# Third token group before the prompt in every stage of an encoder layer, and the prompt's FFN operands kept in DRAM

## The chip, the cores and the metric

The kernel runs on one core of a Trainium2 chip. The metric is the device time of one execution in microseconds (us). Three runs of the kernel before gave 1874.11, 1875.97 and 1880.21 us (median 1875.97 us); the execution that was profiled took 1872.49 us. The engines are named as the profile names them: PE is TensorE (matmul; PEld its weight load), DVE is VectorE, ACT is ScalarE, POOL is GpSimd, SP is SyncE, which issues nearly all DMAs.

## The reference, cut to what matters

One encoder layer with the same weights is applied to a prompt of 1024 tokens and to a sample of 512 tokens; a conditioning vector of each gives its six adaLN vectors. Width is 1024, FFN width 2816, everything in float32.

```
def encoder_layer(x, c, ...):
    mod = silu(c) @ w_ada + b_ada                  # six vectors: sh1 sc1 gt1 sh2 sc2 gt2
    h = rms_norm(x, g_pre_mix) * (1 + sc1) + sh1
    proj = h @ w_in                                # q, k, v of 12 heads x 64; gu, gv of 256 each
    for three dilations (1, 4, 16), 4 heads each:  # 64 strided neighbours on each side, ALiBi
        out[g], lse[g] = dilated_window_attention(q, k, v)
    attn = concat(softmax over g of lse[g] * out[g])
    gm = gelu(gu) * (w_s @ layer_norm(gelu(gv)) + b_s)     # in chunks of 128 positions
    x = x + gt1 * rms_norm(concat(attn, gm) @ w_out, g_post_mix)
    h = rms_norm(x, g_pre_ffn) * (1 + sc2) + sh2
    gate, up = split(h @ w_gu)
    return x + gt2 * rms_norm((silu(gate) * up) @ w_down, g_post_ffn)
```

## The kernel before, in words

Tokens are handled in three groups of 512: groups 0 and 1 are the two halves of the prompt (`self.P`), group 2 is the sample (`self.S`). Activations lie transposed, as 8 chunks of 128 channels by 512 tokens. Every float32 operand of a matmul is split in a high and a low part: `split` (lines 139 to 141) copies on ACT and subtracts on DVE or POOL, and `mm3` does three matmuls for each 128 channels (high by high, high by low, low by high). So a tile of 128 output channels for one group is 24 matmuls of 128x512. Weights come from DRAM through 4 buffers `wraw` and are split into 4 buffers `whl`; one tile's weights take two of each, so that one tile can be prepared ahead. Activations come through 3 buffers `xc` (`load_chunk`). The split activations `h` of a group take 8 of 16 buffers.

The stages of the kernel before run in this order (`run`, lines 1132 to 1204). Statistics of group 0, the first two adaLN vectors (`ada_first`). The prompt's attention slot 0 (`attention_slot`: nine tiles, q, k and v of three dilations, of half of the heads), with the first four tiles' matmuls taken chunk by chunk as `h` of group 0 comes (`project_first`); `gmlp` of groups 0 and 1 (v product, GELU and normalisation on ACT, DVE and POOL, u product, position mixing); the prompt's attention slot 1; the sample's two attention slots; the output projections of groups 0 and 1 (`out_proj`); `gmlp(2)`; the output projection of group 2. Then the prompt's FFN: its up projection (`ffn_up`) multiplies both halves with Strassen-like block products, seven for every 128 hidden channels (`wino_products`), whose right operands are sums and differences of the halves' `h` (called B11, T2, B21, T3, T1, T4, B22). `wino_in` makes them while `out_proj(2)` runs, keeps five of them split in SBUF and two in DRAM (`late`), which `wino_late` brings back. `ffn_down` of groups 0 and 1 follows, and at the end the sample's FFN with plain products (`ffn`, `down`).

Work off the matmul path is written as generators in the list `self.back`; `tick(n)` advances it n steps between tiles, `tick(-1)` empties it. It holds softmax and the value products of a slot (`behind` in `attention_slot`), `mix_in` (loads the mixed outputs of a group and their reciprocal denominators `rden`, multiplies, splits on POOL), the normalisation and residual behind an output projection (`post`), `modulate` (makes `h`). `post` of an FFN that is not the last one sums squares over partitions with `rms_slow` (POOL, then ten instructions on DVE). The last stage has its own ending (`post_last`, lines 888 to 905), which works in halves of the tokens. A scheduler of the framework fixes each engine's order of instructions ahead of the run; on each engine they then run in that order.

Of the kernel before, what the change touches and what calls it, by code (L numbers as in the profile page):

```python
# [9 lines left out]
F32 = mybir.dt.float32  # L10
# [68 lines left out]
class Layer:  # L79
    def __init__(self, tc, ctx, a):  # L80
# [14 lines left out]
        self.late = self.dr.tile([2, 4, 128, TG], F32, name="late")  # L95
# [334 lines left out]
    def project_first(self, grp, tiles, steps):  # L430
# [17 lines left out]
        for hf, gi in enumerate(grp.halves):  # L448
            for i, (w, (_, evac, after)) in enumerate(zip(ws, tiles)):
                if hf:  # L450
                    ps[i] = self.p("mm")
                    self.mm3(ps[i], w, range(KC), self.h[gi])
                self.flush()
                with self.tc.high_priority(offset=1):
                    evac(hf, ps[i])
                if hf:
                    self.tick(steps)
                    self.pending.append(after)
# [259 lines left out]
    def attention_slot(self, grp, sp, steps, between=None, start=None):  # L718
# [22 lines left out]
        if grp is self.P and sp == 0:  # L741
# [3 lines left out]
        if grp is self.P and sp == 0:  # L745
# [90 lines left out]
    def post(self, gi, product, G, xsrc, dst, follow, steps):  # L836
# [3 lines left out]
        last = gi == NG - 1 and not follow  # L840
# [47 lines left out]
    def post_last(self, sq, ys, product, G, xsrc, dst):  # L888
# [4 lines left out]
        for i, ps in enumerate(product(KC - 1, True)):  # L893
            o = slice(256 * i, 256 * i + 256)
            with self.tc.high_priority(offset=1):
                nc.scalar.activation(ys[-1][:, 1, o], ps, AF.Copy, scale=G[:, KC - 1, 1:2])
# [33 lines left out]
    OPS = ["vm"] * 2 + ["v"] * 3 + ["qk"] * 3 + ["sc"] + ["qk"] * 3 + ["h"] * 8  # L930
    HIDP = ["h"] * 8 + ["qk"] * 6 + ["v"] * 3 + ["vm"] * 2 + ["sc"] + ["st"] * 2
# [4 lines left out]
    def wino_in(self, ops):  # L936
# [3 lines left out]
        for o in ("B11", "T2", "B21", "T3", "T1", "T4", "B22"):  # L940
            ops[o] = []
        for k in range(4):
            B = {}
            for kk in range(2):
                pair = self.t("st", [128, 2, 512])
                for gi in range(2):
                    kc = k + 4 * kk
                    x = self.load_chunk(self.x1[gi, :, kc])
                    t = pair[:, gi]
                    nc.vector.tensor_tensor(out=t, in0=x, in1=rs[gi], op=ALU.mult)  # L950
# [325 lines left out]
```

## Time and profile before

| | us |
|---|---|
| runs, median (lowest to highest) | 1875.97 (1874.11 to 1880.21) |
| the profiled execution | 1872.49 |
| its span, first to last instruction | 1870.4 |
| PE busy | 1797.6 (96%) |
| DVE busy | 1051.6 (56%) |
| ACT busy | 692.3 (37%) |
| POOL busy | 123.6 (7%) |
| mean granted clock of TensorE | 0.981 |

The span and the time differ by 2.1 us outside the instructions. PE is busy in 96% of the span, so a reader looks first at where it is not (the stretches with less than 50 us of PE in 50), then at the clock in the same stretches: at 0.5 a matmul takes twice its time and PE still counts as busy.

### The profile page before, as it was taken

The page shows a single profiled execution, that of the slowest core. Times are in us where ns is not written, and L with a number is a line of the kernel's source. Part 1 is how long each engine was busy: PE and PEld are TensorE (multiplying, and loading weights), DVE is VectorE, ACT ScalarE, POOL GpSimd, SP SyncE. Part 2 cuts the span into 40 slices and gives each one's busy share as a digit, 9 for nine tenths or more (in the row PEclk, how much of TensorE's full clock was granted, in tenths as well). Part 3 has the DMA queues.
Part 4 walks back from the last instruction along what each step waited for, and adds up shares of the span by engine and source line. Part 5 has one row for each costly group of instructions (what it writes and reads, how often), then busy time and mean ns, then how long its engine had stood idle before and what let it go on. Part 6 is the DMA issues. An engine that isn't in the chain of part 4 may idle for free.

```text
span 1870.4 us, 22825 instructions
## 1 busy us (share of the span) xinstructions
PE 1797.6 (96%) x8442; PEld 1406.2 (75%) x8442; DVE 1051.6 (56%) x1663; ACT 692.3 (37%) x1196; POOL 123.6 (7%) x82
## 2 busy tenths in 40 slices
PE   6899999999999977889999999999999999999997
PEld 3677876767777866667778888877887888888886
DVE  3424963573675566985566766663375374444223
ACT  4511642162334545642332322343345333333232
POOL 0000100010131003400000000000002000000001
PEclk9899999999999998889999999999999999999999
DMA  9012332233363446553322222264365252222432
GB/s 365 29 56 71 106 114 76 81 129 131 102 202 129 143 164 196 182 201 108 118 94 71 79 91 73 74 205 142 100 209 184 95 170 92 95 96 93 138 93 76
DMA packets 126127, 232.44 MB, mean 124 GB/s; under 512 B 14144, under 2 KB 19520, under 8 KB 126016
## 3 DMA queue, kind: packets, MB, share of 16 engines
q1 hardware_dynamic: 125872, 230.93, 37.0%
q8 instruction: 66, 1.08, 0.2%
q14 instruction: 45, 0.37, 0.1%
q10 hardware_dynamic: 144, 0.07, 0.0%
HBM read 196.86 MB, written 34.08 MB: 123 GB/s over the span
## 4 chain that ended last, share of the span: by engine, by line
PE 51%; issue 3%; DVE 2%; DMA 1%; ACT 0%; POOL 0%; DVEq 0%; POOLq 0%; ACTq 0%
PE pmm L158 44%; PE ppv L158 6%; DMA xc<-hid 1%; PE pst L158 1%; DVE h L141 0%; DVE sc L902 0%; DVE whl L141 0%; DVE sc L861 0%; DMA xc<-late 0%; DVE sc L904 0%; POOL h L141 0%; ACT h L140 0%; DVE v L141 0%; DVE st L1026 0%; DVE qk L141 0%
## 5 line engine op out<-in xcount | busy, mean ns | idle before, releaser
L158 PE MATMUL pmm<-h,whl 128*128 128x512 f32 x3717 | 921.7, 400 | 11.9 <-ACT h L140 6.3
L158 PEld LDWEIGHTS pmm<-h,whl 128*128 128x128 f32 x3717 | 692.4, 190 | 204.1 <-issue 27.4
L141 DVE TENSOR_TENSOR whl<-wraw,whl 128x512 fp32r<-128x512 f32 (+1 forms) x420 | 291.6, 699 | 302.4 <-ACT whl L140 302.1
L140 ACT CAST whl<-wraw 128x512 fp32r<-128x512 f32 (+1 forms) x420 | 252.8, 606 | 495.8 <-PE pmm L158 353.9
L158 PE MATMUL pmm<-qk,whl 128*128 128x512 f32 x798 | 201.7, 397 | 1.2 <-DVE whl L141 1.2
L158 PEld LDWEIGHTS pmm<-qk,whl 128*128 128x128 f32 x798 | 151.0, 190 | 37.2 <-DVE whl L141 2.4
L158 PE MATMUL pmm<-h,sc 128*128 128x512 f32 x411 | 103.8, 397 | 0.0
L158 PE MATMUL ppv<-h,whl 128*128 128x512 f32 x396 | 100.0, 395 | 0.0
L158 PE MATMUL pmm<-v,whl 128*128 128x512 f32 x342 | 90.4, 396 | 0.9 <-ACT whl L140 0.9
L158 PEld LDWEIGHTS pmm<-h,sc 128*128 128x128 f32 x411 | 78.4, 192 | 17.1 <-DVE h L141 0.6
L158 PEld LDWEIGHTS ppv<-h,whl 128*128 128x128 f32 x396 | 74.5, 188 | 18.1 <-issue 0.8
L158 PE MATMUL pst<-qk 64*128 64x128 f32 (+3 forms) x384 | 69.4, 334 | 17.8 <-DVE qk L141 17.5
L158 PEld LDWEIGHTS pst<-qk 64*128 64x128 f32 (+1 forms) x384 | 50.8, 199 | 39.3 <-issue 32.8
L158 PEld LDWEIGHTS pmm<-v,whl 128*128 128x128 f32 x342 | 64.2, 188 | 18.1 <-ACT whl L140 3.0
L158 PE MATMUL pmm<-vm,whl 128*128 128x512 f32 x225 | 65.5, 407 | 4.9 <-ACT whl L140 4.9
L192 DVE TENSOR_TENSOR acc<-acc,ta 128x512 f32<-128x512 f32 x55 | 38.8, 705 | 49.4 <-ACT ta L849 42.7
L140 ACT CAST whl<-sd 128x512 fp32r<-128x512 f32 x53 | 32.7, 619 | 87.2 <-PE ppv L158 52.1
L158 PEld LDWEIGHTS pmm<-vm,whl 128*128 128x128 f32 x225 | 42.4, 192 | 20.9 <-ACT whl L140 6.9
L218 POOL TENSOR_TENSOR rq<-rq,half 128x4 f32<-128x4 f32 (+1 forms) x11 | 12.0, 1091 | 623.1 <-DVE rq L217 623.1
L141 DVE TENSOR_TENSOR whl<-sd,whl 128x512 fp32r<-128x512 f32 x53 | 36.5, 688 | 21.8 <-ACT whl L140 21.7
L848 ACT ACTIVATE sc<-pmm,G 128x512 f32<-128x512 f32 x47 | 32.3, 688 | 41.9 <-PE pmm L158 41.8
L1026 DVE TENSOR_TENSOR st<-st,ppv 128x512 f32<-128x512 f32 x44 | 30.1, 685 | 31.0 <-PE ppv L158 30.7
(249 smaller groups left out, 1929.3 us busy)
## 6 DMA issues: line engine op xcount, KB each, us to landing
wraw<-in_wgu SPq DMA_DIRECT2D x132, 256.0 KB, 2.5
wraw<-in_wdn SPq DMA_DIRECT2D x120, 256.0 KB, 2.6
wraw<-in_win SPq DMA_DIRECT2D x80, 256.0 KB, 2.8
xc<-in_wada SPq DMA_DIRECT2D x48, 256.0 KB, 3.3
wraw<-in_wout SPq DMA_DIRECT2D x48, 256.0 KB, 3.0
sd<-in_wgu SPq DMA_DIRECT2D x44, 256.0 KB, 3.3
xc<-hid SPq DMA_DIRECT2D x44, 256.0 KB, 3.3
xc<-in_x SPq DMA_DIRECT2D x40, 256.0 KB, 3.4
```

The lines of the kernel that those rows point to most:

```text
L140: self.nc.scalar.copy(hi, src)
L141: (eng or self.nc.vector).tensor_tensor(out=lo, in0=src, in1=hi.bitcast(F32), op=ALU.subtract)
L158: self.nc.tensor.matmul(out, lhsT, rhs, start=start, stop=stop, skip_group_check=True)
L192: nc.vector.tensor_tensor(out=acc, in0=acc, in1=t, op=ALU.add)
L218: nc.gpsimd.tensor_tensor(out=y, in0=y, in1=self.half8[:, :n], op=ALU.pow)
L848: nc.scalar.activation(ys[-1][:, mt % 2], ps, AF.Copy, scale=G[:, mt, c:c + 1])
L1026: add = lambda o, a, b: nc.vector.tensor_tensor(out=o, in0=a, in1=b, op=ALU.add)
```

## The change

The sample comes first in each stage. `run` now goes: the sample's slot 0 (with `project_first`), `gmlp(2)`, the sample's slot 1, the prompt's slots 0 and 1, `gmlp(0)`, `gmlp(1)`, the output projections of groups 2, 0 and 1, the sample's FFN, the prompt's `ffn_up`, `ffn_down(0)`, `ffn_down(1)`, which is now the last stage. `wino_in` and `wino_late` become `operands`, which runs in `self.back` during the sample's FFN and stores all seven operands in DRAM (`ops`), and `operands_in`, which loads and splits them: two operands during the sample's down projection, five between it and `ffn_up`. In the prompt's slot 0 the first two tiles, not the last two, are taken together, and `h` of group 1 is finished between their halves (`second_half`). The number of matmuls of each shape is the same.

```diff
@@ project_first
-        for hf, gi in enumerate(grp.halves):
-            for i, (w, (_, evac, after)) in enumerate(zip(ws, tiles)):
...
+        for p, (_, evac, after) in zip(ps, tiles):
+            self.flush()
+            with self.tc.high_priority(offset=1):
+                evac(0, p)
+            self.tick(steps)
+            self.pending.append(after)
@@ attention_slot
         if between:
-            tiles[-2:] = [tiles[-2] + tiles[-1]]
+            tiles[:2] = [tiles[0] + tiles[1]]
         for t in tiles:
-            self.project(grp, t, steps, between if t is tiles[-1] else None)
+            self.project(grp, t, steps, between if t is tiles[0] else None)
@@ post
-        last = gi == NG - 1 and not follow
+        last = gi == 1 and not follow
@@ 
-    OPS = ["vm"] * 2 + ["v"] * 3 + ["qk"] * 3 + ["sc"] + ["qk"] * 3 + ["h"] * 8
+    OPS = ["h"] * 8 + ["v"] * 3 + ["qk"] * 6 + ["vm"] * 2 + ["sc"] + ["h"] * 8
...
-    def wino_in(self, ops):
+    def operands(self):
         rs = [self.spread(self.rs2[gi], True) for gi in range(2)]
+        yield
         for k in range(4):
...
+            a, b = self.t("sd", [128, 3, 512]), self.t("sd", [128, 3, 512])
+            B = {(0, 0): a[:, 0], (0, 1): a[:, 1], (1, 0): a[:, 2], (1, 1): b[:, 0]}
+            for (kk, gi), t in B.items():
+                nc.sync.dma_start(out=t, in_=self.x1[gi, :, k + 4 * kk])
+            yield
+            for (kk, gi), t in B.items():
+                kc = k + 4 * kk
+                nc.vector.tensor_tensor(out=t, in0=t, in1=rs[gi], op=ALU.mult)
+                nc.scalar.activation(t, t, AF.Identity, bias=self.mod[:, 3, kc, 0:1], scale=self.G[2][:, kc, 0:1])
+                if gi:
+                    yield
+            B11, B12, B21, B22, T1, T2 = a[:, 0], a[:, 1], a[:, 2], b[:, 0], b[:, 1], b[:, 2]
+            keep = lambda o, t: nc.sync.dma_start(out=self.ops[o, k], in_=t)
             self.sub(T1, B12, B11)
             self.sub(T2, B22, T1)
+            keep(0, B11)
...
+    def operands_in(self, ops, os):
+        for o in os:
             for k in range(4):
-                x = self.load_chunk(self.late[i, k])
-                h = self.t("h", [128, 2, 512], F32R)
+                x = self.load_chunk(self.ops[o, k])
+                h = self.t(self.OPS[4 * o + k], [128, 2, 512], F32R)
                 self.split(h[:, 0], h[:, 1], x)
                 ops[o].append(h)
+                yield
@@ ffn
-            self.tick(1)
+            self.tick(2)
+        self.back.append(self.operands_in(ops, range(2)))
         self.down(gi, hid)
@@ run
+        self.attention_slot(self.S, 0, STEPS[0], start=start)
+        self.gmlp(2, GS)
+        self.alongside(self.x_stats_behind(self.chunks(self.a["x"][1]), rs, 1))
+        self.attention_slot(self.S, 1, STEPS[1])
+        while 1 not in rs:
+            self.tick(1)
+        self.alongside(self.make_h(1, rs[1], self.chunks(self.a["x"][1]), H2))
+        self.attention_slot(self.P, 0, STEPS[2], second_half)
+        self.attention_slot(self.P, 1, STEPS[3])
         hs = [[], [], []]
+        self.gmlp(0, GS)
+        self.alongside(self.mix_in(2, hs[2]))
+        self.gmlp(1, GS)
+        while len(hs[2]) < KC:
+            self.tick(1)
+        self.back.append(self.mix_in(0, hs[0]))
+        self.out_proj(2, hs[2], 4)
...
+        self.alongside(self.mix_in(1, hs[1]))
+        self.out_proj(0, hs[0], 3)
...
+        self.back.insert(0, self.ffn_in(2, h2))
+        self.out_proj(1, hs[1], 3)
...
+        self.back.append(self.operands())
+        self.ada = self.ada_rest((5,))
+        self.ffn(2, h2, ops)
+        while len(ops[1]) < 4:
+            self.tick(1)
+        for _ in self.operands_in(ops, range(2, 7)):
+            pass
+        self.ffn_up(ops)
+        self.ffn_down(0)
+        self.ffn_down(1)
         self.tick(-1)
```

The change moves instructions on every engine. Three places are shown: first PE at the last gMLP ahead of an output projection. Before, that is `gmlp(2)`; `pmm<-whl,h` is its v product, `pmm<-h,whl` x48 its u product, `pst<-qk` its position mixing, and the next `pmm<-h,whl` the projection of group 2. Before:

```order
L158 MATMUL pmm<-whl,h 128x256 x30
L158 MATMUL pst<-tb,ones 128x128 x4
L158 MATMUL pmm<-h,whl 128x512 x48
L158 MATMUL pst<-qk 128x128 x32
L158 MATMUL pmm<-h,whl 128x512 x8
```

On PE in the changed program, the same place is `gmlp(1)`; `ppv` are value products of the prompt's slot 1.

```order
L158 MATMUL pmm<-h,whl 128x512 x46
L158 MATMUL ppv<-sc,v 64x192 x2
L158 MATMUL ppv<-sc,v 64x256 x4
L158 MATMUL ppv<-sc,v 64x192 x2
L158 MATMUL pst<-qk 128x128 x16
L158 MATMUL pmm<-h,whl 128x512 x9
L158 MATMUL ppv<-sc,ones_82 64x64 x2
L158 MATMUL ppv<-sc,ones_82 64x192 x2
L158 MATMUL ppv<-sc,ones_82 64x256 x4
L158 MATMUL ppv<-sc,ones_82 64x192
L158 MATMUL pst<-qk 128x128 x16
```

Value products and the first matmuls of an output projection now stand between the u product and the position mixing.

The second place is DVE where one pair of attention slots ends and `h` of a group must replace that of the group before it: `L387` and `h<-tb,h` make `h`, `whl` are weight splits. Before, at the end of the prompt's slots:

```order
L141 TENSOR_TENSOR whl<-wraw,whl 128x512 x2
L141 TENSOR_TENSOR h<-tb,h 128x512
L387 TENSOR_TENSOR tb<-xc,rs 128x512
L141 TENSOR_TENSOR h<-tb,h 128x512
L387 TENSOR_TENSOR tb<-xc,rs 128x512
```

On DVE in the changed program, between the sample's slot 1 and the prompt's slot 0; `L589` is the maximum over keys and `L618` the subtraction of it in the softmax of the sample's slot 1:

```order
L141 TENSOR_TENSOR h<-tb,h 128x512
L493 SCALAR_TENSOR_TENSOR sc<-cst,pst 128x512
L387 TENSOR_TENSOR tb<-xc,rs 128x512
L618 TENSOR_TENSOR sc<-sc,st 128x64
L589 TENSOR_TENSOR st<-st,sc 128x4x128
L618 TENSOR_TENSOR sc<-sc,st 128x3x128 x2
L618 TENSOR_TENSOR sc<-sc,st 128x64
L618 TENSOR_TENSOR sc<-sc,st 128x512 x2
L141 TENSOR_TENSOR h<-tb,h 128x512
L141 TENSOR_TENSOR whl<-wraw,whl 128x512
```

The softmax of the slot just ended now stands among the instructions that make `h`, ahead of a weight split.

The third place is DVE at the head of `ffn_up`: `whl` are the split weights of the block products, `x<-xc,x` the split operands. Before, where the two late operands are split:

```order
L141 TENSOR_TENSOR whl<-wraw,whl 128x512 x2
L141 TENSOR_TENSOR whl<-ta,whl 128x512
L141 TENSOR_TENSOR h<-sd,h 128x512
L934 TENSOR_TENSOR wraw<-wraw 128x512
L141 TENSOR_TENSOR h<-st,h 128x512
L934 TENSOR_TENSOR st<-st,sd 128x512
L141 TENSOR_TENSOR h<-xc,h 128x512 x2
```

On DVE in the changed program, at the same place; the split in the first row is that of the first block product's weights, the one in the last row holds the second's:

```order
L141 TENSOR_TENSOR whl<-wraw,whl 128x512
L141 TENSOR_TENSOR qk<-xc,qk 128x512 x3
L141 TENSOR_TENSOR vm<-xc,vm 128x512 x2
L929 TENSOR_TENSOR ta<-wraw 128x512
L141 TENSOR_TENSOR sc<-xc,sc 128x512
L986 TENSOR_TENSOR wraw<-wraw 128x512
L192 TENSOR_TENSOR acc<-acc,ta 128x512
L141 TENSOR_TENSOR h<-xc,h 128x512
L929 TENSOR_TENSOR wraw<-wraw 128x512
L141 TENSOR_TENSOR h<-xc,h 128x512 x2
L141 TENSOR_TENSOR whl<-wraw,whl 128x512 x2
```

Fifteen of the twenty operand chunks that come in from DRAM now stand ahead of the second product's weights (the six rows before these hold the other six).

## Rows read from the trace of the kernel before

**Rows 1.** The page, busy time, share and instructions of each engine.

```profile
PE 1797.6 (96%) x8442; PEld 1406.2 (75%) x8442; DVE 1051.6 (56%) x1663; ACT 692.3 (37%) x1196; POOL 123.6 (7%) x82
```

**Rows 2.** Windows: stretch, its length, busy us of engines, PE clock, DMA share, GB/s.

```profile
0.00:50.00 50.00, 33.52 (x154) 16.87 (x154) 18.96 (x51) 21.80 (x39) 1.45 (x8) 0.96 0.90 341
...
650.00:700.00 50.00, 40.44 (x234) 35.11 (x232) 32.97 (x58) 25.51 (x51) 3.66 (x3) 0.94 0.51 172
700.00:750.00 50.00, 39.17 (x164) 30.46 (x165) 35.52 (x55) 29.11 (x53) 16.93 (x13) 0.82 0.61 192
750.00:800.00 50.00, 39.95 (x162) 30.79 (x160) 46.55 (x67) 33.17 (x61) 21.36 (x10) 0.90 0.59 193
800.00:850.00 50.00, 47.16 (x184) 34.98 (x185) 38.91 (x65) 18.00 (x31) 1.32 (x1) 0.90 0.55 189
...
900.00:950.00 50.00, 50.00 (x224) 38.32 (x223) 31.28 (x60) 16.79 (x29) 0.00 (x0) 1.00 0.33 111
...
1600.00:1650.00 50.00, 50.00 (x217) 40.54 (x216) 20.78 (x32) 16.10 (x27) 0.00 (x0) 1.00 0.27 95
```

**Rows 3.** Waits of PE: on whom, us in total, times, longest.

```profile
PE pst L158 <- DVE qk L141: 17.5, 2, 13.0
...
PE pst L158 <- DVE acc L192: 6.4, 1, 6.4
PE pmm L158 <- ACT h L140: 6.3, 4, 3.9
```

**Rows 4.** Timeline of PE: start, us, instructions, idle before and its end.

```profile
71.35 13.72 PE L158 MATMUL pmm<-h,whl 128*128 128x512 f32 x48 [3.94 <-ACT h L140]
...
679.03 11.41 PE L158 MATMUL pmm<-h,whl 128*128 128x512 f32 x48
703.40 3.64 PE L158 MATMUL pst<-qk 128*128 128x128 f32 x16 [12.96 <-DVE qk L141]
...
801.55 1.22 PE L158 MATMUL pmm<-vm,whl 128*128 128x512 f32 x2 [4.14 <-ACT whl L140]
804.06 5.49 PE L158 MATMUL pmm<-h,whl 128*128 128x512 f32 x12 [1.28 <-DVE st L1026]
```

**Rows 5.** Windows of 10 and 30 us, columns as in rows 2.

```profile
20.00:30.00 10.00, 7.69 (x28) 3.10 (x28) 8.04 (x20) 6.29 (x12) 0.00 (x0) 0.83 1.03 410
...
680.00:710.00 30.00, 14.08 (x61) 11.59 (x60) 28.11 (x52) 15.20 (x28) 3.27 (x2) 0.74 0.60 199
```

**Rows 6.** Groups by form: line, engine, operation, count, busy us, mean ns, idle before.

```profile
L141 DVE TENSOR_TENSOR whl<-wraw,whl 128x512 fp32r<-128x512 f32 x396 | 281.8, 716 | 273.6 <-ACT whl L140 273.3
...
L862 DVE TENSOR_TENSOR sc<-sc,xc 128x512 f32<-128x512 f32 x40 | 26.9, 686 | 14.8 <-DMA xc<-x 8.4 <-DMA xc<-in_x 6.3
L861 DVE TENSOR_TENSOR sc<-sc,rs 128x512 f32<-128x512 f32 x40 | 24.6, 683 | 0.6 <-ACT rs L234 0.6
...
L623 DVE TENSOR_TENSOR sc<-sc,st 128x512 f32<-128x512 f32 x16 | 13.5, 888 | 0.0
L734 DVE RECIPROCAL st<-st 128x1024 f32<-128x1024 f32 x2 | 13.1, 6564 | 0.0
...
L594 DVE TENSOR_TENSOR st<-st,sc 128x512 f32<-128x512 f32 x8 | 9.1, 1157 | 0.1
...
L140 ACT CAST h<-xc 128x512 fp32r<-128x512 f32 x40 | 24.7, 619 | 44.7 <-DVE xc L912 26.6 <-DMA xc<-hid 8.1 <-DMA xc<-late 6.6
```

**Rows 7.** Tile xc, 1222 to 1266 us: issue ns (min/median/max), first and last start.

```profile
L239 SPq DMA_DIRECT2D xc<-hid x26: 319/320/326, 1225.0 to 1263.8; - x26
```

**Rows 8.** DMA issues: count, KB each, median us from issue to landing.

```profile
xc<-rden SPq DMA_DIRECT2D x18, 256.0 KB, 2.8
...
rden<-st SPq DMA_DIRECT2D x6, 256.0 KB, 2.0
```

**Rows 9.** Timeline of POOL: start, us, instructions, idle before and its end.

```profile
711.55 1.27 POOL L141 TENSOR_TENSOR h<-xc,h 128x512 fp32r<-128x512 f32 x1 [4.70 <-ACT h L140]
...
752.20 7.53 POOL L141 TENSOR_TENSOR qk<-st,qk 128x512 fp32r<-128x512 f32 x2 [4.31 <-ACT qk L140]
```

More of the change, by code (lines that the diff above doesn't have):

```diff
@@ L94, in __init__ @@
         self.hid = self.dr.tile([2, NJ, 128, TG], F32, name="hid")
-        self.late = self.dr.tile([2, 4, 128, TG], F32, name="late")
+        self.ops = self.dr.tile([7, 4, 128, TG], F32, name="ops")
         self.h = {}
@@ L740, in attention_slot @@
             tiles.append((9 * sp + 3 * g + 2, evac, after))
-        if grp is self.P and sp == 0:
+        if start:
             tiles = [tiles[i] for i in FIRST]
@@ L744, in attention_slot @@
         tiles = [[t] for t in tiles]
-        if grp is self.P and sp == 0:
+        if start:
             first = self.project_first(grp, [t[0] for t in tiles[:4]], steps)
@@ L1087, in ffn_in, with ffn @@
                                  0 if gi < 2 else 1, hs, H3)
-    def ffn(self, gi, h2):
+    def ffn(self, gi, h2, ops):
         nc = self.nc
@@ L1129, in by_halves @@
                 yield ps[:, 0:256]
-        self.post(gi, product, self.G[3], self.x1[gi], self.a["y"][gi], False, 2 if gi != 1 else 3)
+        self.post(gi, product, self.G[3], self.x1[gi], self.a["y"][gi], False, 2)
     def run(self):
@@ L1142, in run, with prepare @@
             self.raws.append(raw)
-        wa.append(self.ada_load(1))
-        load.append(self.resident(self.a["x"][1], ["v", "v", "v", "sc"]))
-        wa += [self.ada_load(2), self.ada_load(3)]
+        wa += [self.ada_load(ch) for ch in range(1, 4)]
         ada = self.ada_first(wa)
-        rs = {0: self.x_stats(load[0])}
+        rs = {2: self.x_stats(load)}
         for _ in ada:
             pass
+        def prepare(gi):
+            x = self.chunks(self.a["x"][gi])
+            yield from self.x_stats_behind(x, rs, gi)
+            yield from self.make_h(gi, rs[gi], x, H1)
         def start(first):
@@ L1167, in start @@
             self.ada = self.ada_rest((2, 3, 4))
-        def next_group():
-            self.alongside(self.make_h(2, rs[2], self.chunks(self.a["x"][2]), H2))
-            self.tick(NT)
-        for sp in range(2):
-            self.gmlp(sp, GS) if sp else None
-            if sp:
-                self.alongside(self.x_stats_behind(self.chunks(self.a["x"][2]), rs, 2))
-            self.attention_slot(self.P, sp, STEPS[0], next_group if sp else None, None if sp else start)
-            if not sp:
-                self.gmlp(0, GS)
@@ L1179, in run, with second_half @@
-        hs = [[], [], []]
-        for sp in range(2):
-            if sp:
-                self.back.append(self.mix_in(0, hs[0]))
-            self.attention_slot(self.S, sp, STEPS[1])
-        self.tick(-1)
-        self.back.append(self.mix_in(1, hs[1], tags=["qk"] * 6 + ["v"] * 2))
-        self.out_proj(0, hs[0], 4)
-        self.out_proj(1, hs[1], 4)
+            self.back.append(prepare(0))
+        def second_half():
+            while len(self.h[1]) < KC:
+                self.tick(1)
@@ new lines, in run @@
+        self.alongside(self.mix_in(2, hs[2]))
[4 more added lines that the diff above has]
+        self.out_proj(2, hs[2], 4)
+        while len(hs[0]) < KC:
+            self.tick(1)
+        self.alongside(self.mix_in(1, hs[1]))
+        self.out_proj(0, hs[0], 3)
+        while len(hs[1]) < KC or 2 not in self.rs2:
+            self.tick(1)
+        h2, ops = [], [[] for _ in range(7)]
+        self.back.insert(0, self.ffn_in(2, h2))
@@ L1188, in run @@
+        self.out_proj(1, hs[1], 3)
         for _ in self.ada:
             pass
-        self.back.append(self.mix_in(2, hs[2], range(6)))
-        self.gmlp(2, GS)
-        self.tick(-1)
-        for _ in self.mix_in(2, hs[2], range(6, 8)):
-            pass
-        ops, h2 = {}, []
-        self.back.append(self.wino_in(ops))
-        self.out_proj(2, hs[2], 3)
-        self.wino_late(ops)
-        self.ada = self.ada_rest((5,))
+        while len(h2) < KC:
+            self.tick(1)
+        self.back.append(self.operands())
```

80 lines of the change are left out of this document (19 added, 61 removed).

## The prediction

> **What bounds the kernel now.** Read the busy times first: PE is busy in 96% of the span, no other engine in more than 56% [rows 1]. The change leaves the matmuls as they are, so it can only move the time in which PE waits or runs at the half clock. The windows say where that is [rows 2]. From 850 us on PE fills every stretch at clock 1.00, as in 900 to 950; DVE then has 31.3 us of work in 50 in the prompt's `ffn_up`, 20.8 in the sample's FFN. The holes are two. At the start PE has 33.5 us in the first 50. Between 650 and 850 us it lacks 9.6 + 10.8 + 10.0 + 2.8 = 33.3 us, and the clock falls to 0.82.
>
> The waits and the timeline name what makes the second hole. In `gmlp(2)` PE finishes the u product at 679.03 + 11.41 = 690.4 us and has nothing queued that doesn't hang on the normalised v: it waits 13.0 us and again 4.5 (the pair is the 17.5 us of the waits) [rows 3, 4]. Meanwhile DVE is busy for 28.1 us of 30 [rows 5]: it also carries the residual of group 1. Then the head of `ffn_up`: 6.4 us for the square sum of `out_proj(2)`, 4.1 and 1.3 us for split weights [rows 3, 4].
>
> A wait costs more than itself. Behind the 4.1 and 1.3 us, twelve matmuls take 5.49 us, where 48 take 11.41 us at full clock, 2.85 us for twelve; behind the 3.94 us at the start, 48 take 13.72 us [rows 4]. So each gap of about 4 us adds some 2.5 us at half clock. For the five such places of the hole I take 13 us; clock times busy time in the four windows gives at most 2.4 + 7.1 + 4.0 + 4.7 = 18 us [rows 2].
>
> **What goes.** The middle hole, 33.3 + 13 = 46 us: `gmlp(1)` has value products and `out_proj(2)` beside its normalisation, `out_proj(2)` has `out_proj(0)` behind it, and the sample's FFN needs nothing that is made late, since its `h` comes during `out_proj(1)`. At the start, the 2 MB of group 1 no longer stand ahead of the last adaLN weights: at 410 GB/s [rows 5] 5 us. I count 2, since squares of group 0 and weight splits now stand on DVE ahead of the last two chunks of `h`. The wait for `h` of group 1 goes as well, 3.9 us and its 2.3 us of clock [rows 4]. Together 8 us. Gains: 54 us.
>
> **What comes.** Sums over DVE are made instruction by instruction in the changed order, with the durations of the groups (some stand in [rows 6]).
>
> Sample's slot 0 into `gmlp(2)`. Each weight tile now serves 24 matmuls, not 48, while DVE also makes statistics and `h` of group 0, scores and the softmax. Between the last full tile's weights and those of the v product DVE has 22 us of work; PE has 13 us, and 5.6 us of one prepared tile. Gap 3.5 us with clock 2.5: 6 us. Bounds: 0 (DVE was ahead) and 12 (the order's waits for POOL in the softmax fall in it).
>
> Sample's slot 1 into the prompt's slot 0. `h` of group 1 replaces that of group 2 while the softmax of slot 1 stands in the same order: from one half of the second tile's weights to the next lie about 15 us of DVE (the maxima at 1.16 us and the subtractions at 0.89 us are the long ones [rows 6]); PE has two half tiles of 5.6 us and about 5 us of slack. Gap 4, clock 2: 6 us, bounds 0 and 12.
>
> Head of `out_proj(0)`. Its second chunk needs the denominators of the prompt's slot 1. From the last value product: one addition 1.1, reciprocal 6.6, store 2.0, load 2.8, product 0.7, copy 0.6, subtraction on POOL 1.3, together 15 us [rows 6, 8, 9]. PE has two tiles of `out_proj(2)` and a chunk, 12.5 us: 2.5 us are missing. Six chunks follow, each with two loads through three `xc` buffers, about 2.8 us apart, where three tiles side by side give PE 2.1 us a chunk; 4.5 us more. With the clock 9.5 us; bounds 3 and 17.5 (the pair of `gmlp(2)`). Queued behind the reciprocal on DVE are the next weight splits; on SP, behind the store of the denominators, the next `xc` loads. The Trainium skill (SBUF — State Buffer, section "Who interferes with whom") says that a DVE instruction with two SBUF inputs and a GpSimd one that reads SBUF block each other for a whole instruction. The eight POOL splits ahead of `out_proj(2)` show none of it, 1.27 us each; two while the operands are made took 7.5 us [rows 9]. By the rule this term would be up to 9 us dearer, 18.5, and the forecast 9 us later; by the row of the same stage it stays.
>
> Operands. 16 products, 20 differences and 16 activations are moved from beside `out_proj(2)` to the sample's FFN, where DVE idles 29 us in 50 [rows 2] over more than 250 us: 36 times 0.69 us, 25 us, are covered, 0 us on the path; 25 if not. Their 28 stores and the 28 loads are 14.7 MB more on queues that are 27% busy there [rows 2]; a weight load that waits on SP behind such a store costs 0 to 5 us. I take 1.
>
> Head of `ffn_up`. Twenty chunks must be loaded and split after their buffers (`v`, `qk`, `vm`, `sc`, `h`) come free in the last tile of `down`. Loads of this kind went at 38.8/25 = 1.55 us each [rows 7]. Fifteen stand on DVE ahead of the second product's weights; three are prefetched, so twelve take 18.6 us, and one copy and two subtractions 2.0: 20.6 us. PE has 57 matmuls of `down` and 12 of the first product at 0.2375 us, 16.4. The gap is 4 to 7 us, depending on what else stands between; I take 6, and 2.5 for the clock. Then `post` of the sample puts ten instructions of `rms_slow`, eight products and eight sums (0.68 each [rows 6]), some 18 us, among those of the block products, with four weight tiles prepared (11 us): 4.5 us more. Together 13 us. Bounds: 4, and 26 (what stood at this place before: 12.9 us of waits and twice that with the clock).
>
> Smaller transitions (`gmlp(0)` after the prompt's softmax, the sample's FFN beginning under the residual of `out_proj(1)`): 2 us, bounds 0 and 8. The ending is the same code with the prompt's second half.
>
> **Sum.** Against the profiled execution: 1872.5 - 54 + 6 + 6 + 9.5 + 1 + 13 + 2 = 1856.0 us. The median of the runs shown is 3.5 us above that execution, so 1859.5 us; I say 1859. With every cost at its lower bound: 1872.5 - 54 + 7 + 3.5 = 1829; with every one at its upper (12 + 12 + 17.5 + 25 + 5 + 26 + 8 = 105.5), 1927, which would need all at once.
>
> **Rivals.**
> Covered: the prepared weights and the fixed order hide most new waits; only the two heads remain, at 8 us each. For it: from 900 to 950 us PE is full beside a DVE that is busy in 31.3 us of 50 [rows 2]. Against: the long chains end in loads, which no order shortens. 1872.5 - 54 + 16 + 3.5 = 1838.
>
> Moved: the gaps return at their old price, one normalisation without cover and a head of `ffn_up` as before, 54 us in all: 1876. For it: DVE's work is not less, and a fixed order that waits for a load holds all behind it. It is also the case in which the change does not do what it says, the operands' loads taking the place of their making.
>
> The sample's slots at the start, slower: from slot 0 to the prompt's first tile PE has 128 us of matmuls, DVE about 110 us of work in one strict order that also waits for POOL, `xc` loads and PSUM. In 680 to 710 us each wait of a nearly full DVE was PE's [rows 5]. Once DVE's waits there exceed 18 us, DVE sets the pace: with 40 us of waits PE loses 22 us, and nine gaps at 2.5 us of clock add 22; 44 in place of 12. 1859.5 + 32 = 1891. Against it: 110 us of work in 128 leave those 18 us, and 31.3 of 50 left PE full [rows 2].
>
> **How the numbers follow.** Forecast 0.48 (its own range 1848 to 1870), covered 0.22, moved 0.13, slower 0.17. The range that leaves two in ten out goes from 1834 to 1885: it takes in the covered case and the moved one and leaves out most of the slower one. About 0.3%, 5.6 us, is what a measurement of this kernel can tell from no change: under 1870.4 lie the forecast but for its upper edge, and the covered case, 0.70; within 0.3% that edge and most of the moved case, 0.13; slower 0.17.
>
> **What would show it.** In the changed profile, `pst<-qk` no longer heads the waits of PE; in every gMLP the wait ahead of it is under 5 us. Windows with less than 50 us of PE stand at four places: before 60 us, in the sample's first gMLP and the change of `h` (the first 220 us), at the head of `out_proj(0)` with a wait for `h` from POOL or for `xc<-rden`, and at the head of `ffn_up` with a wait for `whl` behind `xc<-ops`. The sample's FFN runs at 50 of 50 and clock 1.00 with more DVE than 20.8. The forecast is wrong if the first 220 us show a clock below 0.9 after 80 us, if the head of `ffn_up` loses more than 26 us, or if PE waits in the sample's FFN.

## The result, and the profile after

| | before | after |
|---|---|---|
| median (lowest to highest), 4 runs each | 1876.24 (1874.11 to 1880.21) us | 1855.20 (1854.07 to 1856.45) us |
| ratio, 95% interval | | 0.9886 (0.9868 to 0.9904) |
| profiled execution, its span | 1872.49, 1870.4 us | 1856.45, 1854.7 us |

The change makes the kernel 21.0 us faster by the medians, 16.0 us by the profiled executions. The forecast was 1859 us. The first row below is the page's line of busy times; beside [rows 1], PE is busy for 12.3 us less with the same instructions, and its idle time falls only from 72.8 to 69.4 us. The spans differ by 15.7 us, so 3.4 us of that are idle time and the rest is busy time. What the half clock costs is half of PE's busy time in the stretches at which it was granted: 39.1 us were busy at half clock before and 28.1 us are now, so 19.5 us were lost and 14.1 us are, 5.5 us less (the longer stretches stand below). The other 6.8 us of busy time went at full clock. Some 6 us of them are the adaLN matmuls, which overlap more than before; the last section has their rows.

```profile
PE 1785.3 (96%) x8442; PEld 1402.8 (76%) x8442; DVE 1049.6 (57%) x1675; ACT 694.3 (37%) x1196; POOL 113.3 (6%) x70
```

The windows of the kernel after, to be set beside [rows 2] (stretch, its length, busy us of PE, PEld, DVE, ACT, POOL, clock, DMA share, GB/s):

```profile
0.00:100.00 100.00, 85.45 (x398) 58.13 (x399) 56.21 (x125) 54.40 (x97) 2.45 (x9) 0.98 0.64 231
100.00:600.00 500.00, 498.71 (x2765) 379.27 (x2764) 283.24 (x455) 179.70 (x293) 58.60 (x24) 1.00 0.30 100
600.00:700.00 100.00, 87.16 (x402) 67.41 (x402) 56.77 (x70) 45.37 (x80) 22.06 (x16) 0.97 0.54 177
700.00:800.00 100.00, 90.44 (x405) 73.54 (x404) 71.54 (x111) 55.96 (x101) 15.10 (x12) 0.93 0.61 201
800.00:1100.00 300.00, 300.00 (x1316) 237.99 (x1315) 136.84 (x222) 111.33 (x191) 1.33 (x1) 1.00 0.47 154
1100.00:1200.00 100.00, 80.54 (x323) 63.84 (x322) 62.28 (x97) 33.18 (x58) 3.50 (x1) 0.90 0.39 124
```

The stretches at half clock, with the same columns, first in the middle hole of the kernel before:

```profile
694.20:718.10 23.90, 10.18 (x39) 9.38 (x40) 17.89 (x35) 9.40 (x16) 5.82 (x4) 0.50 0.67 214
776.20:786.40 10.20, 7.15 (x19) 5.16 (x20) 10.20 (x15) 7.88 (x14) 4.32 (x4) 0.50 0.61 207
800.00:810.30 10.30, 7.46 (x17) 5.38 (x18) 9.91 (x17) 4.79 (x8) 0.00 (x0) 0.50 0.50 174
```

and in the kernel after, from 600 to 1200 us:

```profile
633.50:637.00 3.50, 3.50 (x13) 3.11 (x13) 0.69 (x1) 1.26 (x4) 1.75 (x2) 0.51 0.54 155
664.30:667.70 3.40, 3.40 (x9) 2.61 (x9) 2.29 (x3) 2.11 (x5) 1.27 (x1) 0.50 0.76 229
742.80:756.40 13.60, 6.03 (x14) 4.77 (x15) 10.45 (x18) 7.23 (x13) 0.00 (x0) 0.50 0.69 233
1145.50:1155.80 10.30, 5.94 (x14) 4.68 (x15) 10.30 (x15) 5.65 (x10) 3.50 (x1) 0.50 0.50 160
1183.10:1193.30 10.20, 4.65 (x11) 3.68 (x12) 10.00 (x17) 0.58 (x1) 0.00 (x0) 0.50 0.01 2
```

Read a window's loss as its idle time plus half of the busy time that lies in such stretches. (A wide window's busy time times what its mean clock lacks to 1 is more than that, since much of the half clock falls on waits.) The middle hole of the kernel before lost 33.3 us idle and 12.4 to the clock. After the change the first 100 us lose 14.6 + 1.7 us; the sample's slots, its gMLP and the prompt's slots (100 to 600) 1.3; the output projections (600 to 800) 22.4 + 6.4; the sample's FFN nothing; the head of `ffn_up` (1100 to 1200) 19.5 + 5.3. There are two holes now where there was one.

The waits of PE in the kernel after (on whom, us in total, times, longest). The wait for the normalised v of `gmlp(2)`, 17.5 us in [rows 3], is 0.9 us:

```profile
PE pmm L158 <- ACT ta L844: 11.1, 2, 9.6
PE pmm L158 <- ACT tb L1036: 10.7, 1, 10.7
...
PE pst L158 <- DVE qk L141: 0.9, 1, 0.9
```

The timeline of PE puts them in place (start, us, instructions, idle before and its end): 645 to 664 us is the head of `out_proj(0)`, 750 us is `out_proj(1)`, the last two are the first and the second tile of `ffn_up`.

```profile
645.62 13.75 PE L158 MATMUL pmm<-h,whl 128*128 128x512 f32 x58 [2.54 <-DVE whl L141]
662.27 0.72 PE L158 MATMUL pmm<-h,whl 128*128 128x512 f32 x2 [2.90 <-ACT whl L140]
...
750.37 16.72 PE L158 MATMUL pmm<-h,whl 128*128 128x512 f32 x59 [9.56 <-ACT ta L844]
...
1149.86 1.22 PE L158 MATMUL pmm<-h,whl 128*128 128x512 f32 x2 [8.04 <-ACT whl L140]
...
1188.65 4.21 PE L158 MATMUL pmm<-v,whl 128*128 128x512 f32 x9 [10.71 <-ACT tb L1036]
```

Two of these waits, 9.6 and 10.7 us, name ACT, which was itself held. What ACT waited for, from 690 to 760 us:

```profile
ACT sc L843 <- DMA x<-sc: 2.8, 2, 2.6
```

And from 1170 to 1190 us:

```profile
ACT tb L1036 <- DVE tb L180: 9.4, 1, 9.4
```

`sc` and `tb` are kinds of SBUF tiles, of which there are six and two. The first: a product of `out_proj(1)` can't leave PSUM before an `sc` tile is free, and that tile holds group 0 until its residual is stored. The second: the copy of the second tile's first block product needs one of two `tb` tiles, and `rms_slow` of the sample holds both. So by the code both waits are for a tile and not for ACT's work; the experiments test that.

### The profile page after: what moved, and what is told of

Its sections match the earlier page's. It is cut to its first block, busy times and chain, and to the rows that moved or that the text cites. A ratio compares the mean times of both kernels' runs of the same rounds, so it can differ in the third digit from the quotient of the medians.

```text
span 1854.7 us, 22895 instructions
## 1 busy us (share of the span) xinstructions
PE 1785.3 (96%) x8442; PEld 1402.8 (76%) x8442; DVE 1049.6 (57%) x1675; ACT 694.3 (37%) x1196; POOL 113.3 (6%) x70
## 4 chain that ended last, share of the span: by engine, by line
PE 84%; issue 5%; DVE 5%; DMA 3%; ACT 1%; POOL 1%; SPq 0%; DVEq 0%; ACTq 0%; POOLq 0%
PE pmm L158 69%; PE ppv L158 9%; PE pst L158 6%; DMA xc<-rden 1%; DVE sc L618 1%; POOL st L653 1%; DMA xc<-ops 1%; DVE whl L141 1%; DMA xc<-in_x 0%; DVE sc L856 0%; DMA h<-in_wada 0%; POOL h L141 0%; DMA xc<-mix 0%; DVE sd L618 0%; ACT tb L389 0%
## 5 line engine op out<-in xcount | busy, mean ns | idle before, releaser
L158 PE MATMUL pmm<-h,whl 128*128 128x512 f32 x4008 | 990.4, 401 | 32.6 <-ACT whl L140 11.2
L158 PEld LDWEIGHTS pmm<-h,whl 128*128 128x128 f32 x4008 | 749.8, 190 | 241.6 <-issue 28.7
L158 PE MATMUL pmm<-qk,whl 128*128 128x512 f32 (+1 forms) x570 | 141.1, 394 | 0.0
L158 PEld LDWEIGHTS pmm<-qk,whl 128*128 128x128 f32 x570 | 107.1, 188 | 25.3 <-DVE whl L141 0.3
L158 PE MATMUL pmm<-v,whl 128*128 128x512 f32 x405 | 102.6, 398 | 10.7 <-ACT tb L1036 10.7
L158 PEld LDWEIGHTS pmm<-v,whl 128*128 128x128 f32 x405 | 77.5, 192 | 28.6 <-ACT tb L1036 11.1
L158 PE MATMUL ppv<-h,whl 128*128 128x512 f32 x264 | 65.1, 395 | 0.0
L158 PEld LDWEIGHTS ppv<-h,whl 128*128 128x128 f32 x264 | 49.6, 188 | 11.9
L140 ACT CAST h<-xc 128x512 fp32r<-128x512 f32 x56 | 34.5, 621 | 54.7 <-DVE xc L907 29.9
L653 POOL PARTITION_ALL_REDUCE st<-st x8 | 34.6, 4326 | 317.1 <-DVE st L589 289.2
L493 DVE SCALAR_TENSOR_TENSOR sc<-cst,pst 128x512 f32<-128x512 f32 (+2 forms) x56 | 27.0, 512 | 36.7 <-PE pst L158 31.7
```

What stands on the lines that cost most here:

```text
L140: self.nc.scalar.copy(hi, src)
L158: self.nc.tensor.matmul(out, lhsT, rhs, start=start, stop=stop, skip_group_check=True)
L493: self.nc.vector.scalar_tensor_tensor(out=out, in0=table, scalar=slope, in1=ps, op0=ALU.mult, op1=ALU.add)
L653: self.nc.gpsimd.partition_all_reduce(x[:, :grp.n], x[:, :grp.n], channels=128, reduce_op=RED.max)
```

## The experiments

Each is the kernel after with the edit shown, unless said otherwise. Times are medians, and differences are taken to the 1855.2 us of the kernel after, which was not run again beside them. The kernel before was; by the ratios to it (0.9886 for the kernel after) the differences come out up to 3 us otherwise. Each ratio's interval is some 3 us to either side, so a difference under some 4 us isn't told apart. Of each experiment one execution was profiled.

**The residual of group 0 ahead of the sample's h.**

```diff
-        self.back.insert(0, self.ffn_in(2, h2))
+        self.back.append(self.ffn_in(2, h2))
```

> Only the order of two pieces of background work changes: the residual of out_proj(0) goes ahead of the sample's second h, which stood ahead of it. Buffers theory (the 9.6 us and 1.5 us waits in out_proj(1) are PE waiting for ACT, which waits for an sc buffer that the stores of the late residual of group 0 free): both waits under 2 us together, half clock behind them gone, 11 + 3 us less than the changed kernel, about 1842 us. Rival (the wait only moves: the sample's h comes later and PE waits for it at the head of the sample's FFN): a wait of 8 to 12 us for h there, 1852 to 1857 us.

Measured: 1855.12 us, ratio 0.9894 (0.9879 to 0.9908): no change. From 690 to 800 us PE's waits became three smaller ones and one of 0.4 us:

```profile
PE pmm L158 <- ACT ta L844: 3.5, 1, 3.5
PE pst L158 <- DVE acc L874: 3.0, 1, 3.0
PE pmm L158 <- ACT h L140: 2.0, 1, 2.0
```

The rival had the time right, but not the place: the wait moved, to the squares of group 0 and to `h`, and none stands at the head of the sample's FFN. From 700 to 800 us 5.6 us idle and 5.5 of clock are lost, 11.1 together, where the kernel after lost 9.6 + 3.0 = 12.6: the shorter waits save idle time, and nearly as much goes to the clock. From 600 to 700 us this execution lost 7.8 us to the clock and that of the kernel after 3.4. Six other kernels that share the code of this stage lost 5.0 to 6.7 there, so one profile's clock is good to some 4 us.

**Scratch tiles of the slow inverse root** (`rms_slow`).

```diff
-        self.rsqrt(y, self.t2("tb"), self.t2("tb"), ss, 1.0 / D, RMS_EPS)
+        self.rsqrt(y, ss, self.t2("rs"), ss, 1.0 / D, RMS_EPS)
```

> Only the two scratch tiles of the slow inverse root change: its sum of squares is overwritten and the other comes from rs, so that no tb is held. Buffers theory (the 10.7 us wait in the head of ffn_up is the copy of the second tile's first product waiting for a tb that the inverse root holds, which itself waited for a tb whose store had to land): the wait goes to 0 to 1 us with some 3 us of half clock, about 1842 us. Rival (DVE has too much work there: ten instructions of the inverse root, eight products and eight sums stand ahead of what PE needs whatever the buffers): 5 us or more of waits for DVE between 1175 and 1210 us, 1848 to 1853 us.

Measured: 1843.83 us, ratio 0.9833 (0.9818 to 0.9848), 11.4 us less. Waits of PE from 1100 to 1215 us:

```profile
PE pmm L158 <- ACT whl L140: 6.9, 1, 6.9
PE pmm L158 <- DVE whl L141: 1.8, 1, 1.8
```

The buffers theory holds: DVE's instructions are the same, only the tiles differ, and the 10.7 us wait is gone.

**Operands loaded between the first tile's products.**

```diff
-        for _ in self.operands_in(ops, range(2, 7)):
-            pass
-        self.ffn_up(ops)
+        self.ffn_up(ops, self.operands_in(ops, range(2, 7)))
...                                             # in wino_products, ahead of product o:
             wt = next(w)
+            while len(ops[o]) < 4:
+                next(more)
```

> Only the order changes: the 20 operand chunks that were loaded and split ahead of ffn_up are loaded and split inside its first tile, each product's four just ahead of that product and behind its weights. Order theory (the 8.0 us wait for the second product's weights is their place behind chunks that are not needed yet): that wait goes under 1 us, later chunks cost at most 3 us, about 1847 us. Rival (loads at some 1.5 to 2 us a chunk set the pace): 6 to 10 us of waits for xc<-ops or the operands spread over the first tile's products, 1853 to 1858 us.

Measured: 1852.88 us, ratio 0.9883 (0.9867 to 0.9900), not told apart from the kernel after. The wait for the second product's weights was 5.5 us instead of 8.0. Neither theory was tested: DVE's timeline shows the `qk` and `vm` splits of the operands still ahead of the weights' first difference (L929), so the scheduler kept nearly the old order. Why it did is not shown.

```profile
1139.16 0.69 DVE L141 TENSOR_TENSOR vm<-xc,vm 128x512 fp32r<-128x512 f32 x1 [0.40 <-ACT vm L140]
1139.77 0.69 DVE L929 TENSOR_TENSOR ta<-wraw 128x512 f32<-128x512 f32 x1
```

**Denominators kept in SBUF.**

```diff
+                if grp is self.P and sp:
+                    self.den[gi] = den[:, 512 * hf:512 * hf + 512]
+                else:
                     self.nc.sync.dma_start(out=self.rden[gi, sp], in_=den[:, 512 * hf:512 * hf + 512])
...
-                r = self.load_chunk(self.rden[gi, kc % 2])
+                r = self.den[gi] if kc % 2 and gi in self.den else self.load_chunk(self.rden[gi, kc % 2])
```

> Only the way of the denominators of the prompt's slot 1 changes: they stay in their SBUF tile, and the six chunks of groups 0 and 1 that use them multiply by it; two stores and six loads of 256 KB go. Chain theory (the 11.3 us of waits between 629 and 665 us are the chain reciprocal, store, load, product, and two loads a chunk through three xc buffers): the waits fall to about 4 us, with half clock 9 us less, about 1846 us. Rival (DVE's weight splits and the residual of group 2 behind the reciprocal are what PE waits for): 9 us or more stay, 1853 to 1856 us.

Measured: 1846.14 us, ratio 0.9846 (0.9832 to 0.9861), 9.1 us less. PE's waits from 600 to 690 us, where 11.3 us stood at the head, are this one and 1.8 us of small ones:

```profile
PE pmm L159 <- ACT ta L848: 2.8, 1, 2.8
```

The chain theory holds: the head of `out_proj(0)` was the way of the denominators through DRAM and the two loads a chunk; the edit removes both, so their shares aren't told apart. The 2.8 us is taken for an `sc` wait, which the last experiment bears out.

**The attention's order alone.** The kernel before with the change's attention and gMLP order; `out_proj` in the order 0, 1, 2 and the FFN as before.

```diff
+        self.gmlp(0, GS)
+        self.gmlp(1, GS)
+        self.back.append(self.mix_in(0, hs[0]))
...
         self.out_proj(0, hs[0], 4)
...
         self.out_proj(1, hs[1], 4)
...
         self.back.append(self.wino_in(ops))
         self.out_proj(2, hs[2], 3)
```

> Half of the change: the sample's attention and gMLP stand first, but out_proj goes 0, 1, 2, the operands are made beside out_proj(2) and the FFN comes as in the kernel before (prompt, then sample). Theory that both halves are needed: the start gains its 12 us and the wait for gmlp(2)'s normalisation (17.5 us and some 6 of clock) goes, but the denominators of the prompt's slot 1 now stand right ahead of out_proj(0), with neither out_proj(2) nor anything else beside them: 15 us of chain and six chunks at 3.5 us, less the first tiles, 20 to 30 us of waits; the old head of ffn_up stays. 1875 - 36 + 25 = 1864 us. Rival (the gain is the attention's order alone, the FFN's order gives nothing): 1855 us or less.

Measured: 1874.96 us, ratio 0.9998 (0.9986 to 1.0010): nothing of the gain. Its waits from 560 to 830 us, and its window of 700 to 800:

```profile
PE pmm L158 <- ACT h L140: 17.3, 5, 13.8
PE pmm L158 <- ACT ta L844: 15.1, 1, 15.1
```

```profile
700.00:800.00 100.00, 71.84 (x283) 55.16 (x282) 74.82 (x106) 57.27 (x107) 27.15 (x20) 0.78 0.57 187
```

The start was won as in the change, and lost again at the uncovered head of `out_proj(0)` (13.8 us) and where the operands are made beside `out_proj(2)` (28.2 us idle and 11.4 of clock in 100). So the first half needs the second, as the theory said; it was 11 us too low on the price. The second half alone was not run.

**More work for DVE in the sample's slots.**

```diff
             self.split(w[:, 0, :e], w[:, 1, :e], raw[:, :e], eng)
+            if self.twice:
+                self.sub(w[:, 1, :e], raw[:, :e], w[:, 0, :e].bitcast(F32))
```

> In the sample's two slots and its gMLP every subtraction that splits prepared weights is done twice: 36 more DVE instructions of 0.69 us, 24.8 us, between 40 and 190 us. Theory of the prediction's slower rival (DVE sets the pace there beyond 18 us of waits; 110 us of work in 128): with 25 us more PE loses 7 to 20 us, 1862 to 1875 us. Rival theory (DVE is busy for 88 us of the 130 from 60 to 190 in the changed kernel and its order leaves the rest free): PE loses under 3 us, 1855 to 1858 us.

Measured: 1865.12 us, ratio 0.9955 (0.9938 to 0.9972), 9.9 us more. The waits are at 114 and 118 us, the longer one, 3.7 us, for DVE's split of weights; the window of 100 to 200 us, where PE was full at clock 1.00 after the change:

```profile
100.00:200.00 100.00, 95.14 (x522) 72.83 (x521) 76.78 (x131) 41.64 (x73) 8.35 (x5) 0.97 0.34 111
```

Of 24.8 us added, 4.9 came out as idle time of PE in this window and 3.1 as clock. So some 20 us of room were there, which the change didn't use; beyond it DVE sets the pace.

**Two more MB at the start.**

```diff
-        wa += [self.ada_load(ch) for ch in range(1, 4)]
+        wa.append(self.ada_load(1))
+        self.resident(self.a["x"][1], ["v", "v", "v", "sc"])
+        wa += [self.ada_load(ch) for ch in range(2, 4)]
```

> The 2 MB of group 1 are loaded once more at the start, ahead of the last two chunks of adaLN weights, where they stood before, and not used. DMA theory (the transfers set the pace there, 2 MB at some 400 GB/s): the changed kernel plus 5 us with its clock, 1860 to 1862 us. Rival (DVE and ACT set the pace of the last chunks of h, as the prediction took it): plus 2 us or less, 1855 to 1857 us.

Measured: 1863.63 us, ratio 0.9939 (0.9920 to 0.9957), 8.4 us more. The first 100 us:

```profile
0.00:100.00 100.00, 83.44 (x368) 55.34 (x369) 51.43 (x117) 51.77 (x91) 2.45 (x9) 0.95 0.65 239
```

They lose 16.6 + 4.6 us, 4.9 more than after the change: the DMA theory. The other 3.5 us stand at no one place, and stay open.

**Three edits together**: denominators, inverse root, operands between.

> Three edits together: denominators of the prompt's slot 1 kept in SBUF, the slow inverse root without tb, operands loaded between the first tile's products. If the three waits are separate, the gains add: 1855 - 9 - 11.4 - 2.3 = 1832 us. If one only uncovers another (with the inverse root out of the way the operands' loads between the products come to be waited for, or PE arrives earlier at the sc wait of out_proj(1)), less than 18 us in all: 1837 us or more.

Measured: 1836.61 us, ratio 0.9793 (0.9770 to 0.9815), 18.6 us less: the sum of the first two (20.5), within the noise. The wait for weights was back at 7.6 us, so the third edit had done nothing that lasts.

**Other tiles for out_proj(1).** Six of its chunks leave PSUM into two `sd` tiles, free there.

```diff
-                if mt % 2 == 0:
-                    ys.append(self.t("sc", [128, 2, 512]))
-                nc.scalar.activation(ys[-1][:, mt % 2], ps, AF.Copy, scale=G[:, mt, c:c + 1])
+                if len(Y) == mt:
+                    n = 3 if gi == 1 and follow and mt < 6 else 2
+                    ys.append(self.t("sd" if n == 3 else "sc", [128, n, 512]))
+                    Y.extend(ys[-1][:, i] for i in range(n))
+                nc.scalar.activation(Y[mt], ps, AF.Copy, scale=G[:, mt, c:c + 1])
```

> Only the tiles change in which out_proj(1) leaves six of its eight chunks: two sd tiles, free at that time, in place of three sc tiles; order and work stay. sc theory (out_proj(1) waits for sc tiles that hold group 0 until its residual is stored): the 9.6 us wait of out_proj(1) goes with its half clock, 9 to 12 us less than the changed kernel, 1843 to 1846 us. Rival (what took its place when the residual went first takes it here too: PE waits for the sum of squares of group 0 or for the sample's h): other waits of 5 us or more between 690 and 770 us, 1852 us or more.

Measured: 1850.81 us, ratio 0.9859 (0.9843 to 0.9876), 4.4 us less. The window of 700 to 800 us is full:

```profile
700.00:800.00 100.00, 100.00 (x461) 82.11 (x460) 71.66 (x114) 58.56 (x107) 14.80 (x12) 1.00 0.58 196
```

The `sc` theory holds for the wait, its 9.6 us are gone; half of the expected time doesn't come. The `tanh` of the second tile of the sample's FFN starts at 761.5 us instead of 771.9 on ACT, the first matmul of its `down` at 1012.5 instead of 1016.2. In between PE is full in both kernels, 251.0 and 244.2 us. Of these 6.8 us, 2.0 are 16 small matmuls of square sums that now stand behind the first mark, and 4.9 are the 32 adaLN matmuls in this stretch (24 from `xc`, 8 from `tb`), with which PE is busy for 12.6 us in place of 7.7 (last section).

**The first tile's weights in sd.**

```diff
-            if j % 2 == 0:
+            if j % 2:
                 raw = [self.t2("wraw") for _ in range(4)]
```

> Only the tiles change into which the weights of ffn_up are loaded: even tiles of weights come into sd, odd ones into wraw, so that the first ones are loaded before the last weights of down have left wraw. Theory (the 8.0 us wait is the second product's weights: loaded late through wraw, then placed behind nine operand splits in DVE's order): the wait goes under 2 us, with its clock 8 to 10 us less than the changed kernel, 1845 to 1847 us; the wait for tb stays. Rival (the operand chunks' loads at some 1.3 us each set the pace, whatever the weights do): 5 us or more of waits for h or xc<-ops in the first tile's products instead, 1851 us or more.

Measured: 1852.75 us, ratio 0.9877 (0.9863 to 0.9892), 2.5 us less, not told apart. Waits of PE from 1100 to 1220 us:

```profile
PE pmm L158 <- ACT whl L140: 7.1, 2, 6.6
PE pmm L158 <- ACT tb L1036: 7.1, 2, 6.3
```

The wait at the second product is gone, but a wait of 6.6 us stands 14 us later, near the end of the tile. It names ACT's copy of weights, which stands in ACT's order behind the copies of the last operands, into `h` tiles that `down` leaves last. The timeline of ACT:

```profile
1159.93 0.62 ACT L140 CAST h<-xc 128x512 fp32r<-128x512 f32 x1 [3.05 <-DMA xc<-ops]
1162.19 0.62 ACT L140 CAST h<-xc 128x512 fp32r<-128x512 f32 x1 [1.64 <-DMA xc<-ops]
1162.71 0.61 ACT L140 CAST whl<-wraw 128x512 fp32r<-128x512 f32 x1
```

The rival is right in its cause: the 20 loads set the pace.

**Four edits together**: denominators, inverse root, `sd` for group 1, `sd` for the first tile.

> Four edits together: denominators in SBUF, inverse root without tb, sd for group 1 of out_proj, first tile's weights in sd. If the waits are separate, the gains add: 1855 - 9 - 11.4 - 9 to 12 - 8 to 10 = 1813 to 1818 us. If one uncovers another (the sums of squares of out_proj stand behind the same x loads, DVE carries all of it), 1822 us or more.

Measured: 1830.06 us, ratio 0.9752 (0.9737 to 0.9767), 25.1 us less than the kernel after. The four single gains sum to 9.1 + 11.4 + 4.4 + 2.5 = 27.4, so they add within the noise; the 1813 to 1818 us rested on what the last two were expected to give. One wait for an `sc` tile is left from 600 to 1250 us:

```profile
PE pmm L159 <- ACT ta L850: 4.0, 1, 4.0
```

**The sd tiles for group 0 instead.** As the last, with `gi == 0` in place of `gi == 1`.

> The four edits of before, but the sd tiles take six chunks of out_proj(0) in place of out_proj(1), so that out_proj(0) need not wait for the sc tiles of group 2 nor out_proj(1) for those of group 0. sc theory: the 4.0 us wait at 681 us goes too and none of 9 us comes back, 4 to 6 us less than with the four edits, 1824 to 1826 us. Rival (the 4.0 us were DVE's load with the residual of group 2, whatever the tiles): a wait of 3 us or more stays between 670 and 760 us, 1828 us or more.

Measured: 1828.58 us, ratio 0.9754 (0.9735 to 0.9773): the same as the last. From 600 to 1250 us no wait for `ta` is left; the longest one in the output projections is now:

```profile
PE pst L159 <- DVE acc L880: 2.0, 1, 2.0
```

The 4.0 us wait went, as the `sc` theory says, one of 2.0 us for the squares of group 0 came, and the time didn't move. Both versions beat both kernels by more than their intervals: 2.5% under the kernel before.

## Why the prediction was right, and where only its sum was

The time lies 4 us under the forecast, inside its range, and the sign was the likelier one. Taken term by term, though, the sum is right because errors cancel, and that is luck.

| term | forecast, us | profile, us |
|---|---|---|
| middle hole goes | -46 | -45.7 (33.3 idle, 12.4 clock) |
| start | -8 | -11.3 (27.6 lost before, 16.3 after) |
| the sample's slots and the change of `h` | +12 | +1.3 in all of 100 to 600 |
| head of `out_proj(0)` | +9.5 | +14.7 (11.3 idle, 3.4 clock) |
| smaller transitions, `out_proj(1)` among them | +2 | +14.1 (11.1 idle, 3.0 clock) |
| operands in the sample's FFN | +1 | 0 |
| head of `ffn_up` | +13 | +24.8 (19.5 idle, 5.3 clock) |
| small gaps outside the holes go (4.4 from 100 to 650, 2.5 from 850 to 1800) | none | -6.9 |
| adaLN matmuls overlap more | none | some -6 |

The column sums to some -15; the spans differ by 15.7. The costs came out 17 us above the forecast's 37.5, and what paid for them were 3 us more at the start, the small gaps and the adaLN matmuls. The last of these breaks a premise: "it can only move the time in which PE waits or runs at the half clock" left out that the same matmuls can take less time at full clock when they stand together.

Right: the price of the middle hole, its clock too (13 us taken, 12.4 measured); that the wait for the normalised v ends once something stands beside it; that PE waits nowhere in the sample's FFN though the operands are made beside it; that the denominators' chain is the price at `out_proj(0)`. That last term was 5 us too low, within its bounds (and this profile lost the least clock there of the eight that share the code, by 1.6 to 4.4 us); keeping the denominators in SBUF gave back 9.1 us. Of the four places named for the remaining gaps, three came; the sample's slots have none, and `out_proj(1)` was not named.

Mis-sized, too low and beyond its upper bound: "Smaller transitions", 2 us with "bounds 0 and 8". The step looked at the work under the residual, not at the tiles in which the residual's inputs lie. Six `sc` tiles serve two projections that each want four. With other tiles for one of them the 9.6 us wait went.

Mis-sized, too low, and only just within its upper bound of 26: the head of `ffn_up`. The forecast counted loads and instructions of DVE, and the loads were indeed behind most of the first wait (8.0 us). For `post` of the sample it wrote "4.5 us more" for 18 us of DVE work among the products; with the work as it was and the two `tb` tiles free, 11.4 us went and 1.8 us of waits were left to DVE. So there the tiles were the cause and not the work.

Mis-sized, too high: the sample's slots. The forecast took DVE's order as if each link waited for the next, and gave 12 us to gaps that are not there: PE is full beside a DVE that is busy for 87.8 us of 130.

```profile
60.00:190.00 130.00, 130.00 (x716) 102.01 (x716) 87.76 (x155) 62.28 (x109) 9.23 (x6) 1.00 0.38 125
```

The slower rival rested on the same stretch; it failed on its condition, not its mechanism, which the doubled splits show. Its point, 18 us of waits, is close to the 20 us of room that they found, but it came from 110 us of work in 128, more than the row shows, so this agreement may be chance.

Of the rivals, "covered" wanted 8 us at each head and got 14.7 and 24.8. "Moved" was nearest in kind: it wanted 54 us of new loss, and by the table there are 54.9; its time was wrong because more was gained than it allowed.

At the start the forecast knew the 5 us that 2 MB take and counted 2, as DVE and ACT would be next; the load put back cost 4.9 us there.

On the shared port, the rule of the Trainium skill (SBUF — State Buffer, section "Who interferes with whom") was given up to 9 us at `out_proj(0)`. POOL's splits there took 1.27 to 1.63 us, as without it. The rule shows elsewhere, on DVE's side: a difference of two SBUF tiles that takes 0.68 or 0.69 us elsewhere took 2.73 while POOL summed over partitions, and of the products that make the sample's `h`, of 0.68 us too, one took 1.77 beside POOL's splits. The timeline of DVE, and of POOL:

```profile
724.07 1.77 DVE L387 TENSOR_TENSOR tb<-xc,rs 128x512 f32<-128x512 f32 x1 [1.20 <-POOL h L141]
...
1146.37 2.73 DVE L929 TENSOR_TENSOR wraw<-wraw 128x512 f32<-128x512 f32 x1
```

```profile
722.48 2.81 POOL L141 TENSOR_TENSOR h<-tb,h 128x512 fp32r<-128x512 f32 x2 [2.56 <-ACT h L140]
...
1146.07 3.50 POOL L197 PARTITION_ALL_REDUCE acc<-acc  x1 [326.86 <-DVE acc L192]
```

By that the trace agrees with the rule, at 1 to 2 us a meeting. The meeting of 2.73 us is on the path: ACT's copies of the second product's weights, which PE waits for in its 8.0 us, wait for it. So some 2 of the 8.0 us are the port's, an estimate from these rows.

```profile
1149.19 1.14 ACT L140 CAST whl<-wraw 128x512 fp32r<-128x512 f32 x2 [1.11 <-DVE wraw L929]
```

## What to carry to other kernels

When stages are reordered, list for every tile that work in the background holds which stage will want the same buffers at that time: the two longest new waits here, 9.6 and 10.7 us, were buffers shared by stages that had not met before, and each went when only tiles were changed. A gap costs its idle time and more in clock: over a quarter as much again in the two holes of the kernel after, three quarters from 600 to 800 us where the residual went first, so one long wait split into three short ones may win nearly nothing. Read the clock's cost from the stretches at half clock, and not from a wide window's mean. Half of a reordering can be worth nothing alone, because what it uncovers is what the other half covers.

## What the runs showed of the hardware

The adaLN matmuls, with weights of 32 columns, run side by side when several are issued together. The timeline of PE in the kernel after shows eight of them within 1.1 us (at each of the two starts stands a fourth, with `tb` in place of `xc`), and elsewhere two that take 1.04 us:

```profile
151.72 1.04 PE L158 MATMUL pst<-xc,silz 128*32 128x512 f32 x2
...
189.32 0.63 PE L158 MATMUL pst<-xc,silz 128*32 128x512 f32 x3
...
189.77 0.61 PE L158 MATMUL pst<-xc,silz 128*32 128x512 f32 x3
```

Four start within 0.02 us and the next four 0.45 us later. How much that saves depends on how close together they come. PE's busy time with the 128 of them that come after the first 100 us (stretch, its length, busy us of PE, PEld and DVE, clock, DMA share, GB/s), before the change, after it, and with other tiles for `out_proj(1)`:

```profile
100.00:1871.00 1771.00, 30.55 (x128) 4.22 (x128) 0.00 (x0) 0.98 0.37 121
100.00:1871.00 1771.00, 24.65 (x128) 3.56 (x128) 0.00 (x0) 0.99 0.38 125
100.00:1871.00 1771.00, 29.52 (x128) 4.08 (x128) 0.00 (x0) 0.99 0.38 125
```

So 5.9 us of the change's gain are this, and the other tiles gave 4.9 of them back. No idle time shows it: PE counts as busy either way.
